# Layer 2's modulation on ScalarE and GpSimd over two stages, and every third low part of the weights on GpSimd

## The chip, the cores and the metric

The kernel runs on one core of a Trainium2 chip. The metric is the device time of one execution in microseconds (us); a group of runs is given by its median. The engines are TensorE (PE for its products, PEld for its weight loads), VectorE (DVE), ScalarE (ACT), GpSimd (POOL) and SyncE (SP, whose queue issues all the DMAs here). Each engine works through its own queue in order.

## What is computed

The reference is a two-layer encoder on 1024 tokens of width 1024. In each layer a modulation vector is made from the condition `c`; then come a norm, an input projection, four mixers side by side, an output projection, a second norm and a gated FFN with a short convolution:

```
cond = jax.nn.silu(c)
for l in range(DEPTH):                                  # 2 layers
    mod = cond @ ada_w[l] + ada_b[l]                    # 1024 -> 6 * 1024
    sh1, sc1, g1, sh2, sc2, g2 = jnp.split(mod, 6)
    h = _rms_norm(x, norm1_g[l]) * (1.0 + sc1) + sh1
    pa, pb, pc, pd = _split(h @ w_in[l], GROUP_COLS)
    y = concatenate([rwkv7(pa), diff_attention(pb), gating(pc), forgetting_attention(pd)])
    x = x + g1 * (y @ w_out[l])
    h = _rms_norm(x, norm2_g[l]) * (1.0 + sc2) + sh2
    x = x + g2 * _conv_glu_ffn(h, ffn_up[l], ffn_conv[l], ffn_conv_b[l], ffn_down[l])
```

All of it is float32.

## The kernel before

Tokens are worked on in two halves of 512 (`hf` 0 and 1), layer after layer. A main stage of one half (output projection `wout`, norm, FFN `ffn`, and the next input projection `win`) is written beside the mixers of the other half: `beside(main, mix, units)` takes so many steps of the mixers for each step of the main stage. Three such pairs follow each other: `rest(0,0)` and `win(1,0)` beside `mixers(0,1)`; `rest(0,1)` and `win(1,1)` beside `mixers(1,0)`; `rest(1,0)` beside `mixers(1,1)`. The last stage, `rest(1,1)`, runs alone. Layers are counted 0 and 1 in the code; in this text they are layer 1 and layer 2.

The order of writing gives priorities. The order in which each engine's queue is filled is made when the program is built, by a scheduler that goes through a simulated timeline; on the chip each engine then keeps to it.

**Weights (`wload`, line 491).** Every product of a main stage is made of three passes over weights split into a high part `wh` and a low part `wl` (`acc3`, line 471). One `wload` is a DMA into a raw buffer `wr` (two of them), a cast on ScalarE into `wh`, and a subtraction on VectorE into `wl`; both parts lie in the tile `hr`, three slots of 1024 columns each (`NW = 3`). A load is 1024 columns wide in the input and output projections and in the FFN's `up`, 512 or 384 in `down`.

**Modulation (`ada`, `adav`).** One layer's modulation is 12 groups of 512 outputs. A group is eight loads of 128x512 (`ar`, four buffers), each multiplied by a column of `cond` and summed. Layer 2's groups all go through `adav` (line 383): the even loads on VectorE (a multiplication, then three fused multiply-adds), the odd ones on GpSimd (four multiplications and three additions, lines 397 to 401), a sum of both on VectorE, four one-column products on TensorE into a `pn` tile, and a small addition (`adaout`). All 12 are written beside `rest(0,0)`, one step of a group at every second step of the FFN (`AEV = 2`), and what is left of them ahead of `win(1,0)`. The first norm of layer 2 reads groups 0 to 3, its output projection 4 and 5, its second norm 6 to 9, its FFN 10 and 11.

**Other work on GpSimd.** The FFN's gate has its product `ya * yg` (line 663) and the low part of its result `ml` (line 668) there; the norms have five additions; the mixers have a few clears, copies and parts of the rotation.

## Time and profile before

| | |
|---|---|
| time, median of 3 runs (lowest to highest) | 3023.8 us (3019.92 to 3026.89) |
| profiled execution, its own time | 3017.75 us |
| its span (first to last instruction) | 3016.0 us |
| mean granted TensorE clock, share of full speed | 0.963 |
| busy: PE, PEld, DVE, ACT, POOL | 95%, 80%, 69%, 45%, 20% |

The span is what the profile's views divide up; the profiled execution's own time is 1.75 us longer than it. A busy share is an average over stages that differ, so the views by window and the chain of work that ended last are read stage by stage. Busy time of TensorE counts pipelined products, so a busy TensorE is not one at its peak.

### The profile page before, as it was taken

To read this page: it belongs to the slowest core of one execution; us is meant where nothing else is said; L and a number is where in the kernel's file an instruction comes from. 1 tells how busy PE (TensorE), PEld (TensorE's weight loads), DVE (VectorE), ACT (ScalarE), POOL (GpSimd) and SP (SyncE) were. 2 spreads that over 40 slices of the span, in tenths; PEclk is the share of its full clock that TensorE was granted. 3 is DMA by queue.
4 is the path that set the end of the run, shared out by engine and by line. 5 is a ranking of instruction groups with operands and counts; after the bars stand their busy time and mean duration, and the time that the engine had idled before them with its cause. 6 is when DMAs were issued, how large, how long until landed. Compare 5 with 4: busy or idle time off the path is not lost.

```text
span 3016.0 us, 49828 instructions
## 1 busy us (share of the span) xinstructions
PE 2871.6 (95%) x17816; PEld 2419.6 (80%) x17816; DVE 2073.8 (69%) x4737; ACT 1361.4 (45%) x2760; POOL 609.2 (20%) x660
## 2 busy tenths in 40 slices
PE   7998989899889999999999999999999999999999
PEld 5987887777777888987888887888878888878887
DVE  4678777789886765668775665668787755565555
ACT  3455444444354544444644433455455445343333
POOL 2016253366511110100111111000111111111111
PEclk8999987989989999999999999999999999999999
DMA  7558455455532425463432324453332332523332
GB/s 271 146 164 292 154 169 181 136 163 175 181 98 70 142 85 168 144 188 112 128 109 94 98 75 160 147 170 115 104 113 76 118 109 90 187 59 110 111 95 73
DMA packets 276662, 405.78 MB, mean 135 GB/s; under 512 B 74560, under 2 KB 148800, under 8 KB 276416
## 3 DMA queue, kind: packets, MB, share of 16 engines
q1 hardware_dynamic: 276416, 402.61, 43.0%
q8 instruction: 141, 2.31, 0.3%
q14 instruction: 105, 0.86, 0.1%
HBM read 343.47 MB, written 59.02 MB: 133 GB/s over the span
## 4 chain that ended last, share of the span: by engine, by line
PE 75%; DVE 9%; DMA 7%; ACT 3%; issue 2%; SPq 2%; POOL 1%; DVEq 0%; ACTq 0%; POOLq 0%
PE pm L186 60%; PE pa L186 4%; PE px L186 4%; PE S L186 2%; PE px L1115 2%; DMA ar<-in_ada 2%; DVE hr L189 1%; DMA raw<-pA 1%; PE pn L186 1%; DVE cst L195 1%; DVE cst L189 1%; ACT hr L497 1%; SPq L980 1%; DMA qkB<-qh 1%; DVE cst L1093 1%
## 5 line engine op out<-in xcount | busy, mean ns | idle before, releaser
L186 PE MATMUL pm<-hh,hr 128*128 128x512 f32 (+1 forms) x3328 | 1091.1, 402 | 14.1 <-ACT hh L198 7.3
L186 PEld LDWEIGHTS pm<-hh,hr 128*128 128x128 f32 (+1 forms) x3328 | 627.2, 190 | 155.4 <-ACT hh L198 10.8
L497 ACT CAST hr<-wr 128x1024 fp32r<-128x1024 f32 (+2 forms) x496 | 427.1, 863 | 593.1 <-PE pm L186 484.0
L189 DVE TENSOR_TENSOR hr<-wr,hr 128x1024 fp32r<-128x1024 f32 (+2 forms) x496 | 515.1, 1039 | 249.9 <-ACT hr L497 232.8
L186 PE MATMUL pm<-hl,hr 128*128 128x512 f32 (+1 forms) x1664 | 666.8, 401 | 3.8 <-DVE hl L195 3.8
L186 PE MATMUL pm<-mh,hr 128*128 128x512 f32 x1408 | 460.2, 398 | 3.8 <-ACT p L198 2.8
L186 PE MATMUL pm<-hr,hh 128*128 128x256 f32 x2048 | 399.2, 291 | 7.4 <-DVE hr L189 6.0
L186 PEld LDWEIGHTS pm<-hl,hr 128*128 128x128 f32 (+1 forms) x1664 | 316.2, 190 | 72.5 <-DVE hl L195 6.6
L186 PEld LDWEIGHTS pm<-hr,hh 128*128 128x128 f32 x2048 | 325.6, 193 | 13.5 <-DVE hr L189 6.7
L663 POOL TENSOR_TENSOR y<-y,y 128x512 f32<-128x512 f32 x88 | 116.1, 1320 | 993.7 <-DVE y L189 335.2
L186 PEld LDWEIGHTS pm<-mh,hr 128*128 128x128 f32 x1408 | 266.0, 190 | 59.5 <-ACT p L198 3.3
L195 DVE SCALAR_TENSOR_TENSOR y<-pm,cst,y 128x511 f32<-128x511 f32 x352 | 261.1, 743 | 67.5 <-ACT y L198 64.1
L186 PE MATMUL pm<-hr,hl 128*128 128x256 f32 x1024 | 294.5, 288 | 0.0
L186 PE MATMUL pm<-ml,hr 128*128 128x512 f32 x704 | 277.1, 394 | 0.0
L195 DVE SCALAR_TENSOR_TENSOR x<-pm,cst,x 128x512 f32<-128x512 f32 x224 | 167.2, 747 | 138.3 <-PE pm L186 137.3
L198 ACT ACTIVATE p<-S,cst 128x512 f32<-128x512 f32 (+3 forms) x288 | 165.3, 580 | 90.8 <-DVE cst L189 66.5
L1093 DVE TENSOR_REDUCE cst<-S 128x1 f32<-128x512 f32 (+3 forms) x288 | 153.8, 550 | 70.1 <-PE S L186 69.0
L186 PEld LDWEIGHTS pm<-hr,hl 128*128 128x128 f32 x1024 | 198.1, 193 | 1.3 <-issue 0.7
L186 PEld LDWEIGHTS px<-V,ct 128*128 128x128 f32 x1152 | 160.0, 205 | 30.7 <-ACT ct L1117 22.0
L186 PE MATMUL px<-V,ct 128*128 128x64 f32 x1152 | 162.1, 285 | 17.9 <-ACT ct L1117 17.7
L186 PE MATMUL pm<-yh,hr 128*128 128x512 f32 x512 | 168.2, 405 | 3.9 <-ACT yh L621 3.1
L198 ACT ACTIVATE y<-pm,cst 128x512 f32<-128x512 f32 x176 | 136.6, 776 | 77.9 <-PE pm L186 77.5
(239 smaller groups left out, 3967.7 us busy)
## 6 DMA issues: line engine op xcount, KB each, us to landing
wr<-in_up SPq DMA_DIRECT2D x176, 512.0 KB
ar<-in_ada SPq DMA_DIRECT2D x192, 256.0 KB
wr<-in_wint SPq DMA_DIRECT2D x64, 512.0 KB
wr<-in_down SPq DMA_DIRECT2D x128, 256.0 KB
wr<-in_wout SPq DMA_DIRECT2D x32, 512.0 KB
wr<-in_win SPq DMA_DIRECT2D x28, 512.0 KB
ks<-qkB SPq DMA_DIRECT2D x192, 64.0 KB
wr<-in_down SPq DMA_DIRECT2D x64, 192.0 KB
```

The costliest lines, as they stand in the source:

```text
L186: return self.nc.tensor.matmul(out, lhsT, rhs, start=start, stop=stop, **kw)
L189: self.nc.vector.tensor_tensor(out=out, in0=a, in1=b, op=op)
L195: self.nc.vector.scalar_tensor_tensor(out=out, in0=a, scalar=s, in1=b, op0=op0, op1=op1)
L198: self.nc.scalar.activation(out=out, in_=in_, func=func, **k)
L497: self.nc.scalar.copy(out=h, in_=r)
L663: nc.gpsimd.tensor_tensor(out=ya, in0=ya, in1=yg, op=ALU.mult)
L980: nc.sync.dma_start(out=D[o:o + 16, :, c:c + 16], in_=XB[b0:b0 + 4].rearrange("b i t -> i b t"))
L1093: nc.vector.tensor_reduce(out=nm[:, i:i + 1], in_=S_[:, 0:n], axis=AX.X, op=ALU.max, negate=True)
L1115: nc.tensor.transpose(ps[:, j:j + 128], pc[:, j:j + 128], self.ident)
```

## The change

Three things are changed. Layer 2's groups go through a new `adaw`: all eight multiplications of a group on ScalarE and the seven additions on GpSimd, with one accumulator in place of two. The 12 groups are written in two stages: 0 to 3 beside `rest(0,0)` at every fifth step, 4 to 11 beside `rest(0,1)` at every second (`NA1, E1, E2 = 4, 5, 2`). And from the first of the three pairs to the end of the third (`K.lop = LOP` up to `K.lop = 0`), every third `wload` has its subtraction on GpSimd.

```
@@ -241,6 +241,7 @@
         self.identR, self.mDR, self.mBR = (hr[:, i * 128:i * 128 + 128] for i in range(3))
         self.wh, self.wl = ([hr[:, o + i * 1024:o + i * 1024 + 1024] for i in range(NW)] for o in (384, 384 + NW * 1024))
         self.nw = 0
+        self.npl, self.lop = 0, 0
         nc.vector.tensor_copy(self.identR, self.ident)
         for n, r in (("mD", self.mDR), ("mB", self.mBR)):
             t = self.ntile([128, 128], name="mt")
@@ -383,6 +384,9 @@
     def adav(self, l, g, pool, tag, apn):
 
         nc = self.nc
+        if l:
+            yield from self.adaw(l, g, pool, tag, apn)
+            return
         accs = [self.page(self.an, "an", [128, 512], F32, "av") for _ in range(2 if KD < 8 else 1)]
         new = [True, True]
         for kp in range(4):
@@ -407,6 +411,26 @@
             self.tt(accs[0], accs[0], accs[1], ALU.add)
         for u in range(4):
             self.mm(ps[:, u:u + 1], accs[0][:, u * 128:u * 128 + 128], self.ones[:, 0:1], True, True)
+        self.adaout(l, g, ps)
+
+    def adaw(self, l, g, pool, tag, apn):
+
+        nc = self.nc
+        acc = self.page(self.an, "an", [128, 512], F32, "av")
+        for k in range(8):
+            r = pool.tile([128, 512], F32, name="ar", tag=tag)
+            nc.sync.dma_start(out=r, in_=self.a["ada"][l, g, k // 2][:, k % 2 * 512:k % 2 * 512 + 512])
+            c = self.cond[:, k, 0:1]
+            if k == 0:
+                nc.scalar.mul(acc, r, c)
+            else:
+                nc.scalar.mul(r, r, c)
+                nc.gpsimd.tensor_tensor(out=acc, in0=acc, in1=r, op=ALU.add)
+            if k % 2:
+                yield
+        ps = (self.normps() if apn else self.pm.tile([128, H], F32, name="pm", tag="pm"))
+        for u in range(4):
+            self.mm(ps[:, u:u + 1], acc[:, u * 128:u * 128 + 128], self.ones[:, 0:1], True, True)
         self.adaout(l, g, ps)
 
     def adaout(self, l, g, ps):
@@ -495,7 +519,9 @@
         r = self.wr.tile([128, 1024], F32, name="wr", tag="wr")[:, 0:n]
         self.nc.sync.dma_start(out=r, in_=src)
         self.nc.scalar.copy(out=h, in_=r)
-        self.tt(lo, r, h.bitcast(F32), ALU.subtract)
+        self.npl += 1
+        e = self.nc.gpsimd if self.lop and self.npl % self.lop == 0 else self.nc.vector
+        e.tensor_tensor(out=lo, in0=r, in1=h.bitcast(F32), op=ALU.subtract)
         return h.rearrange("p (k c) -> p k c", k=nk), lo.rearrange("p (k c) -> p k c", k=nk)
 
     def product(self, w, acts, m=128):
@@ -1478,20 +1504,20 @@
                 side(oth, EARLY)
         drain(mix)
         xs[0] = K.load_x(0, True)
-        later = K.ada(1, range(NADA, 12), K.ar, "ar", APN)
-
-        def first():
-            for i, _ in enumerate(rest(0, 0)):
-                if i >= AST and (i - AST) % AEV == 0:
+        K.lop = LOP
+        def with_ada(main, groups, every):
+            later = K.ada(1, groups, K.ar, "ar", APN)
+            for i, _ in enumerate(main):
+                if i >= AST and (i - AST) % every == 0:
                     side(later, 1)
                 yield
             drain(later)
-            yield from win(1, 0)
-
-        beside(first(), K.mixers(0, 1, oth), U1)
+
+        beside(chain(with_ada(rest(0, 0), range(0, NA1), E1), win(1, 0)), K.mixers(0, 1, oth), U1)
         K.layer_params(1)
-        beside(chain(rest(0, 1), win(1, 1)), K.mixers(1, 0), U2)
+        beside(chain(with_ada(rest(0, 1), range(NA1, 12), E2), win(1, 1)), K.mixers(1, 0), U2)
         beside(rest(1, 0), K.mixers(1, 1), U3)
+        K.lop = 0
         K.out_x(0, xs[0])
         xs[1] = K.load_x(1)
         drain(rest(1, 1))
@@ -1500,6 +1526,8 @@
 
 U1, U2, U3 = 90, 60, 80
 MIX0 = 7
+NA1, E1, E2 = 4, 5, 2
+LOP = 3
 
 
 def chain(*gs):
```

How this stands in the queues is shown at three places. The first is ScalarE's queue where the FFN of layer 1 half 0 begins: `y_6773` and `y_6778` are the first pair of up products on their way out of PSUM, `hr` the casts of the weights, `p`, `ct`, `VS`, `yB` the mixers. Before:

```order
L198 ACTIVATE y_6773<-pm,cst 128x512
L497 CAST hr<-wr 128x1024
L198 ACTIVATE y_6778<-pm,cst 128x512
L892 COPY Y<-pa 128x128
L198 ACTIVATE th<-y_6778 128x512
L198 ACTIVATE gsq<-Y 128x256
L667 CAST mh<-th 128x512
L1117 COPY ct<-px 128x512
L1117 COPY ct<-px 128x256
L198 ACTIVATE p,cst<-S,cst 128x512
L198 ACTIVATE p,cst<-S,cst 128x384
L497 CAST hr<-wr 128x1024
```

And with the change, where the lines of the new function are 425 and 427, and the cast of the weights is line 521:

```order
L198 ACTIVATE y_6773<-pm,cst 128x512
L521 CAST hr<-wr 128x1024
L198 ACTIVATE y_6778<-pm,cst 128x512
L427 ACTIVATE ar<-ar,cst 128x512
L916 COPY VS<-pa 64x128
L427 ACTIVATE ar<-ar,cst 128x512
L198 ACTIVATE yB<-px,cst 128x64
L198 ACTIVATE p,cst<-S,cst 128x512
L198 ACTIVATE p,cst<-S,cst 128x256
L427 ACTIVATE ar<-ar,cst 128x512
L425 ACTIVATE av<-ar,cst 128x512
L198 ACTIVATE th<-y_6778 128x512
```

Multiplications of the modulation now stand between the drains of the products, the casts and the mixers' work.

The second place is GpSimd's queue at the same point, from one gate product (`y_6773`) on. Lines 397, 400 and 401 are the modulation before, 663 and 668 the gate. Before:

```order
L663 TENSOR_TENSOR y_6773<-y_6773,y_6778 128x512
L400 TENSOR_SCALAR ar<-ar,cst 128x512 x2
L668 TENSOR_TENSOR ml<-th,mh 128x512
L401 TENSOR_TENSOR av<-av,ar 128x512 x2
L400 TENSOR_SCALAR ar<-ar,cst 128x512
L397 TENSOR_SCALAR av<-ar,cst 128x512
L400 TENSOR_SCALAR ar<-ar,cst 128x512
L401 TENSOR_TENSOR av<-av,ar 128x512
L400 TENSOR_SCALAR ar<-ar,cst 128x512
L401 TENSOR_TENSOR av<-av,ar 128x512
L663 TENSOR_TENSOR y_6886<-y_6886,y_6916 128x512
```

With the change (line 428 is the modulation's addition, 524 the low part of a weight, 689 and 694 the gate):

```order
L689 TENSOR_TENSOR y_6773<-y_6773,y_6778 128x512
L428 TENSOR_TENSOR av<-av,ar 128x512
L694 TENSOR_TENSOR ml<-th,mh 128x512
L428 TENSOR_TENSOR av<-av,ar 128x512 x7
L524 TENSOR_TENSOR hr<-wr,hr 128x1024
L428 TENSOR_TENSOR av<-av,ar 128x512
L689 TENSOR_TENSOR y_6879<-y_6879,y_6909 128x512
L428 TENSOR_TENSOR av<-av,ar 128x512 x3
L694 TENSOR_TENSOR ml<-th,mh 128x512
```

The multiplications are gone from this queue, additions stand in their place, and a low part of the weights stands behind eight of them. Of the six groups that this order puts into the first stage, two stand ahead of the norm and four here; the other six are in the second stage.

The third place is GpSimd's queue in the FFN of layer 1 half 1. Before, it holds the gates alone:

```order
L663 TENSOR_TENSOR y_15350<-y_15350,y_15380 128x512
L668 TENSOR_TENSOR ml<-th,mh 128x512
L663 TENSOR_TENSOR y_15519<-y_15519,y_15549 128x512
L668 TENSOR_TENSOR ml<-th,mh 128x512
L663 TENSOR_TENSOR y_16233<-y_16233,y_16263 128x512
```

With the change it holds additions of layer 2's modulation between two gate products, and low parts among them:

```order
L689 TENSOR_TENSOR y_15283<-y_15283,y_15313 128x512
L428 TENSOR_TENSOR av<-av,ar 128x512
L694 TENSOR_TENSOR ml<-th,mh 128x512
L428 TENSOR_TENSOR av<-av,ar 128x512
L524 TENSOR_TENSOR hr<-wr,hr 128x512
L428 TENSOR_TENSOR av<-av,ar 128x512 x6
L524 TENSOR_TENSOR hr<-wr,hr 128x512
L428 TENSOR_TENSOR av<-av,ar 128x512 x6
L524 TENSOR_TENSOR hr<-wr,hr 128x1024
L428 TENSOR_TENSOR av<-av,ar 128x512 x7
L689 TENSOR_TENSOR y_16043<-y_16043,y_16073 128x512
```

Between these two gate products, 21 additions and three low parts have come in. In the whole order 117 low parts stand on GpSimd: 68 of 1024 columns, 32 of 512, 16 of 384 and one of 32.

## Rows read from the trace of the kernel before

**Rows 1.** The page of the kernel before, its first lines: the span, and for each engine the busy time, its share of the span and the number of instructions.

```profile
span 3016.0 us, 49828 instructions
PE 2871.6 (95%) x17816; PEld 2419.6 (80%) x17816; DVE 2073.8 (69%) x4737; ACT 1361.4 (45%) x2760; POOL 609.2 (20%) x660
```

**Rows 2.** The view by windows, all engines: us of the stretch, its length, then for PE, PEld, DVE, ACT and POOL the busy us (instructions), then the granted TensorE clock as a share of full speed, the DMA engines' busy share and GB/s. The stretches are output projection of layer 1 half 0 (482 to 559), the first and the second half of its FFN (559 to 850, 850 to 1145), the FFN of layer 1 half 1 (1395 to 1840), of layer 2 half 0 (2091 to 2595) and of layer 2 half 1 (2650 to 3016).

```profile
482.00:559.00 77.00, 73.50 (x508) 62.05 (x506) 56.83 (x137) 33.47 (x66) 19.97 (x19) 0.97 0.56 173
...
559.00:850.00 291.00, 261.89 (x1431) 213.34 (x1431) 260.24 (x528) 124.14 (x268) 157.92 (x103) 0.93 0.49 156
...
850.00:1145.00 295.00, 282.74 (x1749) 233.53 (x1748) 203.73 (x522) 144.44 (x318) 40.46 (x43) 0.97 0.36 107
...
1395.00:1840.00 445.00, 438.45 (x2530) 359.46 (x2530) 305.04 (x667) 207.72 (x411) 70.56 (x67) 0.99 0.35 109
...
2091.00:2595.00 504.00, 497.55 (x2925) 411.49 (x2926) 357.08 (x819) 251.46 (x526) 63.92 (x62) 0.98 0.36 109
...
2650.00:3016.00 366.00, 361.28 (x1584) 298.36 (x1584) 213.45 (x307) 132.75 (x185) 57.36 (x44) 0.99 0.30 90
```

**Rows 3.** The same view of one stretch inside the FFN of layer 2 half 0.

```profile
2100.00:2200.00 100.00, 98.00 (x556) 80.42 (x555) 81.64 (x194) 51.07 (x109) 14.13 (x14) 0.98 0.33 102
```

**Rows 4.** The view by windows of the instructions on the tile `pm` alone (the main products in PSUM and what drains them); columns PE, PEld, DVE, ACT, then clock, DMA share and GB/s.

```profile
559.00:850.00 291.00, 203.44 (x771) 148.49 (x771) 47.56 (x85) 18.02 (x24) 0.93 0.49 156
...
1395.00:1840.00 445.00, 387.38 (x1584) 293.27 (x1584) 100.50 (x135) 34.20 (x44) 0.99 0.35 109
...
2091.00:2595.00 504.00, 394.99 (x1585) 292.85 (x1586) 103.02 (x179) 34.10 (x44) 0.98 0.36 109
...
2650.00:3016.00 366.00, 361.28 (x1584) 298.36 (x1584) 101.75 (x136) 34.09 (x44) 0.99 0.30 90
```

**Rows 5.** The chain that ended last, its shares by line, in the stretches 559 to 850, 1395 to 1840 and 2091 to 2595, in this order.

```profile
by line: PE pm L186 23.8%; DMA ar<-in_ada 8.4%; issue 7.6%; DVE hr L189 6.9%; DVE cst L195 4.3%; DVE y L195 4.0%; PE px L186 2.8%; DVE av L403 2.7%; DVE cst L1093 2.6%; DVE cst L189 2.6%; PE pa L186 2.4%; DVE p L195 2.4%; POOL av L401 2.0%;
...
by line: PE pm L186 78.8%; PE pa L186 5.9%; PE px L186 3.1%; PE S L186 2.3%; PE px L1115 1.5%; DMA wr<-in_win 1.1%; issue 1.0%; DVE hl L195 0.7%; SPq L980 0.7%; DVE ht L195 0.6%; DVE hr L189 0.5%; DVE cst L189 0.5%; DMA D<-XB 0.4%; DVE x L1
...
by line: PE pm L186 68.2%; PE px L186 7.6%; PE pa L186 5.2%; PE S L186 4.8%; PE px L1115 3.5%; DMA wr<-in_wout 1.1%; DVE hl L195 1.0%; DVE hr L189 0.9%; issue 0.7%; DMA pc<-pC 0.7%; DVE ht L195 0.7%; DVE cst L1093 0.6%; DMA D<-XB 0.5%; DVE 
```

**Rows 6.** Pieces of that chain in the stretch 559 to 850, in order of time: start, us, what.

```profile
593.54 2.81 DMA ar<-in_ada
...
608.21 3.16 DMA ar<-in_ada
...
691.22 4.80 DMA ar<-in_ada
```

**Rows 7.** The instructions on the tiles `av` and `ar` (layer 2's modulation) and on `wr` (the weights as they land) in the stretch 559 to 850: line, engine, operation, tile, count, ns min/median/max of one, first and last start, forms.

```profile
L401 POOL TENSOR_TENSOR av<-av,ar x33: 1259/1374/2252, 562.7 to 825.7; 128x512 f32<-128x512 f32 x33
...
L403 DVE SCALAR_TENSOR_TENSOR av<-ar,cst,av x30: 735/748/1764, 592.8 to 819.5; 128x512 f32<-128x512 f32 x30
...
L397 POOL TENSOR_SCALAR av<-ar,cst x11: 1557/1643/2308, 561.1 to 806.8; 128x512 f32<-128x512 f32 x11
...
L189 DVE TENSOR_TENSOR av<-av x11: 675/679/1724, 586.2 to 830.5; 128x512 f32<-128x512 f32 x11
...
L397 DVE TENSOR_SCALAR av<-ar,cst x10: 441/474/777, 590.0 to 812.4; 128x512 f32<-128x512 f32 x10
...
L400 POOL TENSOR_SCALAR ar<-ar,cst x30: 1562/1615/3009, 570.9 to 822.6; 128x512 f32<-128x512 f32 x30
...
L189 DVE TENSOR_TENSOR hr<-wr,hr x42: 669/1208/2285, 558.2 to 846.5; 128x1024 fp32r<-128x1024 f32 x25, 128x512 fp32r<-128x512 f32 x17
```

**Rows 8.** Groups of instructions over the whole span, shapes apart: line, engine, operation, tiles, out<-in, count, then busy us and mean ns of one, then idle time of the engine just before them and what ended it. The first two are the low parts of the weights.

```profile
L189 DVE TENSOR_TENSOR hr<-wr,hr 128x1024 fp32r<-128x1024 f32 x300 | 374.4, 1248 | 227.6 <-ACT hr L497 212.5 <-ACT yD L198 5.4 <-PE px L1115 4.4
...
L189 DVE TENSOR_TENSOR hr<-wr,hr 128x512 fp32r<-128x512 f32 x128 | 101.5, 793 | 17.4 <-ACT hr L497 16.6
...
L663 POOL TENSOR_TENSOR y<-y,y 128x512 f32<-128x512 f32 x88 | 116.1, 1320 | 993.7 <-DVE y L189 335.2 <-DVE cst L657 329.5 <-ACT p L198 50.7
...
L198 ACT ACTIVATE sq<-x 128x512 f32<-128x512 f32 x88 | 54.7, 631 | 78.4 <-DMA x<-pD 32.6 <-DVE x L195 17.0 <-DMA x<-pB 15.5
...
L198 ACT ACTIVATE hh<-ht,cst 128x512 fp32r<-128x512 f32 x64 | 44.9, 722 | 49.5 <-DVE ht L195 43.3 <-DMA x<-in_xT 3.5 <-DVE cst L189 2.4
```

**Rows 9.** Waits in the stretch 559 to 850: the engine and line that waited, what for, us in total, times, longest. The two that begin with SPq are the DMA queue's own.

```profile
POOL ar L400 <- DMA ar<-in_ada: 54.1, 16, 11.7
...
PE pn L186 <- DVE av L189: 3.1, 3, 2.1
...
SPq L392 <- POOL av L401: 31.4, 17, 4.6
...
SPq L392 <- DVE av L403: 19.1, 11, 8.4
```

**Rows 10.** The largest wait of ScalarE's casts of the weights, over the whole span.

```profile
ACT hr L497 <- PE pm L186: 484.0, 258, 6.6
```

**Rows 11.** The timeline of TensorE at a modulation group's last four products (each in two passes) and what follows them: start, us, what.

```profile
577.22 0.95 PE L186 MATMUL pn<-cst,av 128*128 128x1 f32 x8
...
578.09 0.45 PE L186 MATMUL pa<-Us,Xs 64*64 64x64 f32 x8
```

**Rows 12.** One group of VectorE over the whole span that reads one operand from PSUM and one from SBUF, as a view by tile has it (count, ns min/median/max).

```profile
L195 DVE SCALAR_TENSOR_TENSOR x<-pm,cst,x x224: 717/751/753, 499.5 to 3012.4; 128x512 f32<-128x512 f32 x112
```

## The prediction

> **What bounds the kernel now.** I read the page first: TensorE is busy 95% of the span, VectorE 69%, ScalarE 45%, GpSimd 20% [rows 1]. So the first question is where TensorE's missing time lies. The view by windows answers it [rows 2]: in the FFN of layer 1 half 1 TensorE idles 445 - 438.5 = 6.5 us, in that of layer 2 half 0 504 - 497.6 = 6.4 us, in the last one 4.7 us. The first half of the first FFN, 559 to 850, is different: 291 - 261.9 = 29.1 us idle, the granted clock is 0.93 of full speed (so part of the stretch ran at 1.2 and not 2.4 GHz), and VectorE is busy 260.2 of 291 us, 89%. Layer 2's modulation runs there. The second half of that FFN has 12.3 us idle.
>
> The chain that ended last says the same [rows 5]. In the two later FFNs the main products hold 78.8% and 68.2% of it. In 559 to 850 they hold 23.8%; the loads of the modulation hold 8.4%, VectorE's low parts 6.9%, its share of the modulation 2.7%, GpSimd's 2.0%.
>
> What would that stretch take if only TensorE set the pace? The last FFN runs alone: 366 us for 1584 main products, 0.231 us each [rows 2, 4]. In the FFN of layer 2 half 0 the 1585 main products at that price take 366 us, and the other 2925 - 1585 = 1340 products the remaining 138 us, 0.103 us each. For 559 to 850 this gives 771 x 0.231 + 660 x 0.103 = 246 us. So some 45 us of 291 come from the other engines, and the change can win little elsewhere.
>
> **The change part by part.** The sum is made against the profiled execution, 3017.75 us; the runs' median, 3023.8 us, lies 6.05 us above it, and that is added at the end.
>
> *VectorE in 559 to 850.* The modulation leaves it: 30 x 0.748 + 10 x 0.474 + 11 x 0.679 = 34.6 us [rows 7]. Of 42 low parts (25 wide, 17 half) a third go: 8 x 1.248 + 6 x 0.793 = 14.7 us [rows 7, 8]. VectorE keeps 260.2 - 49.3 = 210.9 us.
>
> *TensorE there.* Of 96 one-column products, 64 move to the next stage with groups 4 to 11 (the order of the change has 4 groups' products ahead of layer 2's first norm). Eight take 578.09 - 577.22 = 0.87 us [rows 11], so 8 x 0.87 = 7 us leave: 246 becomes 239 us.
>
> *GpSimd there.* The modulation's 33 x 1.374 + 11 x 1.643 + 30 x 1.615 = 111.9 us go [rows 7]. Four groups' 28 additions come, 28 x 1.374 = 38.5 us, and 14 low parts. No GpSimd operation of 1024 columns is in the trace; the nearest, a two-input operation of 512, takes 1.320 us [rows 8]. The wide one lies between 1.3 (all of it fixed) and 2.64 us (none fixed). I take 2.64, as I see no fixed part: 8 x 2.64 + 6 x 1.32 = 29 us. GpSimd falls from 157.9 to 113.5 us. This engine is relieved too, for the four multiplications per group went to ScalarE.
>
> *ScalarE there.* Four groups bring 32 multiplications. Nearest rows: 0.631 us (one operand, constant scale) and 0.722 us (an operand per partition) [rows 8]; I take the second, as `cond` is such an operand: 23 us on top of 124.1.
>
> *What this gives.* VectorE's 210.9 us need room: the highest share it has beside a TensorE at 98% is 81.6% [rows 3], and 210.9 / 0.816 = 258 us. That is later than TensorE's 239, so VectorE still paces the stretch, and I get 33 us of the 45. Something is given back on ScalarE: its queue now meets the modulation's loads itself. GpSimd waited 54.1 us for them over its 41 multiplications [rows 7, 9], 1.3 us each; 32 on ScalarE are up to 42 us. Behind each wait stand casts of weights and drains of products. ScalarE has 258 - 147 = 111 us idle, so I let one fifth reach the path, 8 us. Term: **-25 us**, bounds -52 (TensorE's price) and -6 (below).
>
> *482 to 559.* Two groups' 16 multiplications (11.6 us on ScalarE, busy 33.5 of 77) and 14 additions (19 us) with three low parts on GpSimd stand ahead of the norm's additions. **+2 us**, 0 to +8: the norm waits at most for the end of that row.
>
> *850 to 1145.* VectorE loses the low parts of a third of the weights, at most 17 x 1.248 = 21 us of 203.7. Idle is 12.3 us [rows 2]. **-3 us**, -8 to 0.
>
> *The FFN of layer 1 half 1.* TensorE is full there, and 7 us of one-column products come to it. In the first FFN TensorE waited 3.1 us for three of the sums [rows 9]; here the sum is GpSimd's, at the end of a queue. GpSimd gets 42 x 1.374 = 58 us of additions, and between two gate products 21 of them with three low parts: 21 x 1.374 + 2.64 + 2 x 1.32 + 1.32 = 35.5 us, while the eight `down` products of that place take TensorE 8 x 12 x 0.231 = 22 us and the mixers beside them more. A low part behind such additions can be late by up to 13 us. VectorE, relieved by some 28 us, gives back nothing that TensorE waits for (its low parts hold 0.5% of the chain [rows 5]). **+8 us**, 0 to +22.
>
> *The other low parts.* 117 subtractions leave VectorE in all. A cast into a slot waits for TensorE to finish with it, 484.0 us in 258 waits [rows 10]; the two other slots are full then, 2 x 24 x 0.231 = 11 us of products for wide loads, 5.5 us in `down`. A wide low part later by 2.64 - 1.25 = 1.4 us, a half one by 0.5 us, is hidden by that. If a norm or a pair of products empties the slots, it costs the 1.4 us, some four times. **0 us**, -5 to +8.
>
> Sum: -25 + 2 - 3 + 8 + 0 = -18; 3017.75 - 18 = 2999.75, and with 6.05 **3005.8 us**.
>
> **The rivals.**
>
> *The queues of ScalarE and GpSimd hold the products (slower).* A low part of the weights stands in GpSimd's queue behind additions, these wait for ScalarE, which waits for a load; a load took 2.8 to 4.8 us on the chain [rows 6], and its buffer comes free only with the addition. For it: the SP queue waited 31.4 us for GpSimd's additions [rows 9], and the order has up to seven additions ahead of a low part. Against it: GpSimd has less to do in 559 to 850 than before. Price: two thirds of ScalarE's 42 us reach the path there, 27 us in place of 8 (term -6), and the other ends are +8, 0 for 850 to 1145 and +22: +24 with the rest at 0, 3017.75 + 24 + 6.05 = 3047.8 us. It is slower than before from about 18 us of such waits beyond my own terms.
>
> *VectorE isn't what holds 559 to 850.* Its busy share is then only company, and the pace comes from loads and from round trips of the mixers: "issue" and loads hold 7.6 and 8.4% of the chain, more than VectorE's low parts and modulation together (9.6%). Then only part of the modulation's own chain goes: -10 + 2 + 0 + 8 = 0, 3023.8 us.
>
> *The shared port.* VectorE's operations with two operands in SBUF are stretched when GpSimd runs: the fused multiply-add on `av` has a median of 0.748 and a maximum of 1.764 us, while one that reads PSUM and SBUF has 0.751 and 0.753 [rows 7, 12]. The stretch, 1.0 us, is within a GpSimd operation of 1.3; one of 2.64 us could hold VectorE twice as long. If each of the 117 takes back on average what it relieves, VectorE keeps 225.6 us in 559 to 850, 225.6 / 0.816 = 276 us: -15 + 8 = -7 there, and the small operations of the mixers, held up to 2.6 us, cost 4 us in each later FFN: -7 + 2 + 0 + 8 + 8 = +11, 3034.8 us. The Trainium skill, page "SBUF — State Buffer", section "Who interferes with whom", has this as its rule: a GpSimd operation that reads SBUF and a VectorE operation with two SBUF inputs lock each other out for a whole instruction. By that rule the time is this rival's; the two maxima agree with it. Against the price: GpSimd's total busy time falls in the one stretch where VectorE is short.
>
> *All of the 45 us.* TensorE sets the pace in 559 to 850 (-52), 850 to 1145 gives -8, the second stage costs +5: -55, 2968.8 us. For it: a faster stretch also has the clock that it lacks (0.93 against 0.98).
>
> **How the numbers follow.** Forecast 0.42, queues 0.22, not VectorE 0.15, port 0.08, all of it 0.13. The likeliest is the forecast, 3006 us, alone 2990 to 3020. The range of 8 in 10 reaches into the neighbours: down to 2980 (most of the last rival lies below) and up to 3034 (half of the first rival and half of the port's above). About 0.2%, 6 us, is what a measurement of this kernel can tell from no change: faster is below 3017.8, slower above 3029.8. Faster: 0.38 of the forecast, 0.13, and 0.04 of "not VectorE", 0.55. Slower: 0.20 of the queues and 0.05 of the port, 0.25. The rest, 0.20, is the same.
>
> **What would show it.** In the profile of the changed kernel the stretch from the first `up` product, as long as 1431 - 64 products, should take some 266 us with VectorE at 79% and TensorE's idle time near 12 us. The wide low part on GpSimd should take 2.6 us; at 2.0 us the queue rival weakens. ScalarE's multiplications should idle some 30 to 40 us for loads. The FFN of layer 1 half 1 should take some 453 us; at 465 us, with TensorE waiting for `hr` released by GpSimd, the first rival holds. VectorE's small operations at 1 us and more would speak for the port. The prediction is wrong if the first FFN keeps its 586 us, or if the second stage loses what the first wins.

## The result and the profile after

| kernel | median | runs | ratio to before |
|---|---|---|---|
| before | 3021.9 us | 4 (3016.1 to 3026.9) | 1 |
| changed | 3060.1 us | 4 (3057.6 to 3065.2) | 1.013 [1.0109, 1.015] |

Slower by 38 us; 3006 was forecast, with 3034 as the upper end. The profiled run has a span of 3060.3 us, 44.3 more than before. First the head of the page after; it answers to [rows 1].

```profile
span 3060.3 us, 49880 instructions
...
PE 2880.4 (94%) x17816; PEld 2419.2 (79%) x17816; DVE 2025.3 (66%) x4560; ACT 1418.3 (46%) x2856; POOL 815.3 (27%) x777
```

VectorE did lose work, but less than was taken from it. At the prices of [rows 7, 8], an estimate, layer 2's modulation is some 41 us on VectorE and the 100 larger low parts are 110 us; its busy time fell by 48.5 (2073.8 to 2025.3 us). GpSimd gained 206 us. The same view by windows as in [rows 2], for the stretches that answer to those: output projection and norm, first FFN up to 850 and as a whole, norm and input projection of layer 2 half 0, FFN of layer 1 half 1, FFN of layer 2 half 0.

```profile
494.00:581.00 87.00, 80.97 (x511) 66.62 (x509) 57.87 (x129) 31.03 (x58) 26.35 (x23) 0.89 0.48 148
581.00:850.00 269.00, 251.38 (x1409) 205.12 (x1407) 210.16 (x469) 150.14 (x317) 98.64 (x71) 0.97 0.41 124
...
581.00:1137.00 556.00, 526.25 (x3091) 431.13 (x3090) 408.76 (x959) 287.69 (x617) 169.14 (x130) 0.97 0.39 114
1137.00:1324.00 187.00, 172.22 (x1287) 154.44 (x1286) 107.97 (x267) 87.40 (x171) 31.75 (x24) 0.94 0.51 161
1405.00:1876.00 471.00, 451.27 (x2582) 367.68 (x2580) 307.76 (x635) 231.65 (x452) 180.15 (x139) 0.98 0.41 125
2133.00:2638.00 505.00, 495.57 (x2931) 407.91 (x2930) 355.39 (x791) 248.49 (x526) 115.94 (x92) 0.99 0.36 108
```

The first FFN gained what was forecast: 556 us for 585 (559 to 1144 in before), -29. The rest lost 73: +12 up to the output projection (its order is changed too, and the first low part of GpSimd starts at 431.9 us), +10 in it and its norm, +16 in 1137 to 1324, +28 in the FFN of layer 1 half 1 (471 us for the 443 from 1395 to 1838), +7 in the others together. Inside that FFN the loss lies in its first 150 us. The same view there:

```profile
1405.00:1430.00 25.00, 19.02 (x113) 15.43 (x112) 22.26 (x44) 13.64 (x29) 9.19 (x8) 0.81 0.61 176
1475.00:1500.00 25.00, 18.40 (x84) 13.99 (x84) 24.66 (x51) 10.32 (x23) 13.76 (x10) 0.91 0.31 94
1500.00:1525.00 25.00, 25.00 (x150) 20.66 (x150) 13.71 (x31) 17.61 (x37) 18.48 (x14) 0.95 0.61 189
1525.00:1550.00 25.00, 20.54 (x97) 16.62 (x96) 24.84 (x46) 15.66 (x26) 18.66 (x13) 0.93 0.59 203
1550.00:1575.00 25.00, 25.00 (x126) 21.15 (x125) 16.48 (x34) 12.91 (x29) 9.01 (x6) 1.00 0.45 129
```

Where TensorE is short, VectorE is full (24.66 and 24.84 of 25 us) with only 51 and 46 operations; in before it had 77 in a window of 25 us as full, and TensorE was hardly short:

```profile
1475.00:1500.00 25.00, 24.32 (x118) 19.89 (x117) 24.94 (x77) 12.67 (x29) 2.61 (x2) 1.00 0.30 89
```

Of TensorE's waits in 1405 to 1555, 18.1 of 20.2 us are for steps of VectorE, of the FFN (`y`), a norm and the mixers, and none for weights. The three longest (what it waited for, us in total, times, longest):

```profile
PE pm L186 <- DVE y L189: 6.1, 1, 6.1
PE pa L943 <- DVE Y L189: 4.1, 1, 4.1
PE pa L186 <- DVE cst L189: 3.1, 1, 3.1
```

VectorE's and GpSimd's rows of the timeline there (start, us, what):

```profile
1481.14 1.31 POOL L428 TENSOR_TENSOR av<-av,ar 128x512 f32<-128x512 f32 x1
...
1481.24 1.22 DVE L195 SCALAR_TENSOR_TENSOR cst<-cst 128x4 f32<-128x4 f32 x1
...
1482.40 1.30 POOL L524 TENSOR_TENSOR hr<-wr,hr 128x512 fp32r<-128x512 f32 x1
...
1482.72 2.23 DVE L189 TENSOR_TENSOR cst<-cst 128x4 f32<-128x4 f32 x2
...
1484.99 0.16 DVE L195 SCALAR_TENSOR_TENSOR cst<-cst 128x4 f32<-128x4 f32 x1
...
1487.86 6.34 POOL L428 TENSOR_TENSOR av<-av,ar 128x512 f32<-128x512 f32 x4
...
1487.96 3.45 DVE L189 TENSOR_TENSOR Vn<-Vn,cst 128x512 f32<-128x512 f32 x2
```

The same multiply-add of four columns takes 1.22 us at 1481.24, beside an addition of GpSimd, and 0.16 at 1484.99, where GpSimd rests. Two `Vn` products, 0.745 us each on average in before, take 3.45 beside GpSimd's additions, and the FFN's `y`, for which a TensorE product waited 6.1 us until 1496.3, stands behind such products in VectorE's queue. So VectorE is held up: its operations take longer beside GpSimd's. But `Vn` is held as long with no low part on GpSimd (982 ns on average in e1 below, 996 here), so these rows don't tell which part of the change costs the 38 us. The groups over the whole span, shapes apart; they answer to [rows 7, 8]:

```profile
L524 DVE TENSOR_TENSOR hr<-wr,hr 128x1024 fp32r<-128x1024 f32 x232 | 297.6, 1283 | 210.5 <-ACT hr L521 197.0 <-ACT yD L198 6.3 <-PE px L1141 3.6
...
L524 POOL TENSOR_TENSOR hr<-wr,hr 128x1024 fp32r<-128x1024 f32 x68 | 165.4, 2432 | 635.6 <-ACT hr L521 590.9 <-PE pm L186 34.7 <-PE S L186 9.9
...
L428 POOL TENSOR_TENSOR av<-av,ar 128x512 f32<-128x512 f32 x84 | 115.5, 1375 | 95.6 <-ACT av L425 65.6 <-ACT ar L427 26.0 <-PE pm L186 0.3
...
L427 ACT ACTIVATE ar<-ar,cst 128x512 f32<-128x512 f32 x84 | 59.4, 723 | 51.9 <-DMA ar<-in_ada 51.0 <-POOL av L428 0.7
...
L524 POOL TENSOR_TENSOR hr<-wr,hr 128x512 fp32r<-128x512 f32 x32 | 43.7, 1366 | 86.0 <-ACT hr L521 69.6 <-PE S L186 16.1 <-POOL Xs L1029 0.2
```

### The profile page after: what moved, and what is told of

Its sections match the earlier page's. It is cut to its first block, busy times and chain, and to the rows that moved or that the text cites. A ratio compares the mean times of both kernels' runs of the same rounds, so it can differ in the third digit from the quotient of the medians.

```text
span 3060.3 us, 49880 instructions
## 1 busy us (share of the span) xinstructions
PE 2880.4 (94%) x17816; PEld 2419.2 (79%) x17816; DVE 2025.3 (66%) x4560; ACT 1418.3 (46%) x2856; POOL 815.3 (27%) x777
## 4 chain that ended last, share of the span: by engine, by line
PE 69%; DVE 12%; DMA 8%; ACT 4%; issue 2%; SPq 2%; POOL 2%; ACTq 0%; DVEq 0%; POOLq 0%
PE pm L186 56%; PE pa L186 4%; PE px L186 4%; PE S L186 2%; PE px L1141 2%; DVE hr L524 2%; DVE cst L189 1%; DMA ar<-in_ada 1%; ACT hr L521 1%; DMA raw<-pA 1%; POOL av L428 1%; DMA wr<-in_win 1%; DVE y L195 1%; PE pn L186 1%; DVE cst L195 1%
## 5 line engine op out<-in xcount | busy, mean ns | idle before, releaser
L524 DVE TENSOR_TENSOR hr<-wr,hr 128x1024 fp32r<-128x1024 f32 (+2 forms) x379 | 403.8, 1066 | 237.0 <-ACT hr L521 223.1
L524 POOL TENSOR_TENSOR hr<-wr,hr 128x1024 fp32r<-128x1024 f32 (+3 forms) x117 | 226.8, 1938 | 784.9 <-ACT hr L521 716.6
L189 DVE TENSOR_TENSOR cst<-cst 128x1 f32<-128x1 f32 (+5 forms) x552 | 135.5, 255 | 74.4 <-ACT p L198 62.2
```

Of the source, the lines that this page charges most:

```text
L189: self.nc.vector.tensor_tensor(out=out, in0=a, in1=b, op=op)
L524: e.tensor_tensor(out=lo, in0=r, in1=h.bitcast(F32), op=ALU.subtract)
```

## The experiments

In the table below, all times are against runs of the kernel before on the same chip (3018.7 to 3022.4 us).

| run | what it is | us | ratio |
|---|---|---|---|
| e1 | new modulation in two stages, no low part on GpSimd | 3023.6 | 1.0011 [0.9993, 1.003] |
| e2 | old modulation, low parts on GpSimd | 3055.2 | 1.0119 [1.0096, 1.0143] |
| e3 | new modulation, one stage | 3021.1 | 0.9997 [0.9981, 1.0012] |
| e4 | old modulation, two stages | 3019.1 | 0.9996 [0.9979, 1.0013] |
| f1 | e1, GpSimd only waits at the cast | 3019.9 | 1.0002 [0.9986, 1.0017] |
| f2 | e1, GpSimd reads and subtracts beside | 3053.9 | 1.0106 [1.0081, 1.0131] |
| h1 | e1, GpSimd writes instead | 3012.9 | 0.9972 [0.9954, 0.9989] |
| f3 | changed, low parts in halves | 3015.7 | 0.9981 [0.9968, 0.9993] |
| h2 | changed, low parts in quarters | 3018.3 | 0.9985 [0.9969, 1.0001] |
| h3 | as f3, second half first | 3036.5 | 1.0053 [1.0034, 1.0071] |
| g1 | e2 with halves | 3031.2 | 1.0039 [1.0027, 1.0052] |
| g2 | f3, the modulation's additions in halves too | 3015.7 | 0.9998 [0.9985, 1.0011] |
| g4 | f2 with halves | 3048.1 | 1.0095 [1.008, 1.011] |
| f4 | e1, multiplications and additions on 8 columns | 2990.0 | 0.9902 [0.988, 0.9924] |
| g3 | e1, additions alone on 8 columns | 3009.2 | 0.9958 [0.9942, 0.9973] |

**Which part costs.** Four kernels with one part each.

```diff
e1  -LOP = 3
    +LOP = 0
e2  -NA1, E1, E2 = 4, 5, 2        (and adav runs its old form in layer 2 too)
    +NA1, E1, E2 = 12, 2, 2
e3  -NA1, E1, E2 = 4, 5, 2        -LOP = 3
    +NA1, E1, E2 = 12, 2, 2       +LOP = 0
e4  -LOP = 3                      (and adav runs its old form in layer 2 too)
    +LOP = 0
```

In the expectations, theory S blames the second stage, L the low parts on GpSimd, O the new order of the queues.

Expected of e1: 

> The changed kernel without the low parts on GpSimd (all on VectorE again): the new modulation in two stages alone. Theory S (the second stage is the cause: layer 2's additions on GpSimd and its multiplications on ScalarE in the full FFN of layer 1 half 1 hold VectorE's small operations and the casts): it stays slow, 3050 to 3060 us, and the FFN of layer 1 half 1 takes some 470 us as in the changed kernel. Theory L (the low parts on GpSimd are the cause): it is faster than before, some 3005 us, with that FFN at 445 to 455 us. Theory O (a new order of all queues moves time at places that the change does not touch): 3020 to 3050 us, with the loss spread over stretches without modulation.

Of e2: 

> The kernel before with every third low part on GpSimd and nothing else. Theory S: 3010 to 3025 us, since GpSimd's low parts hide behind the slots; the FFN of layer 1 half 1 at 445 us. Theory L: 3040 to 3060 us. Theory O: within 15 us of before either way, with the difference in the projections and norms more than in the FFNs.

Of e3: 

> The new modulation (multiplications on ScalarE, additions on GpSimd) for all 12 groups in the first stage at every second step, as before, and no low parts on GpSimd: the engines alone. Theory S: faster than before, 2995 to 3010 us, since the first FFN is relieved on VectorE by 35 us and the second stage is left alone. Theory L says the same. If the multiplications on ScalarE are themselves the cause (its queue waits for the loads), it is 3030 us or more with the first FFN at 585 us or longer.

Of e4: 

> The old modulation (VectorE and GpSimd) written in two stages, 0 to 3 and 4 to 11, and no low parts on GpSimd: the split alone. Theory S with the stage as the cause whatever the engine: 3035 to 3055 us, the FFN of layer 1 half 1 at 465 us or more. If it is the new engines in the full stage and not the stage: 3010 to 3025 us. Theory L: 3005 to 3020 us.

The low parts alone (e2) cost 1.2%, about all of the 1.3; the modulation in either form and place costs and gains nothing. So theory S falls, and O by e2, which it had put within 15 us of before. L is right about what costs, but not about the rest: it had expected e1 at some 3005 us and e3 at 2995 to 3010, and the gain that the low parts were thought to hide isn't there. Where that comes from shows in the starts of ScalarE's 496 casts of weights, of which every kernel has the same; the figures are us later (+) or earlier (-) than in before:

```
cast number     64     96    128    160    192    224    288    480
start before   628    827   1038   1230   1471   1636   1942   2965
changed      +16.6   +4.4  -10.7   -4.9  +17.5  +37.5  +41.8  +44.4
e1           +16.5   +1.2  -21.3  -23.7  -15.4   +3.3   +4.6   +4.3
e2           +10.5  +12.1   -6.4   +0.9  +22.2  +31.8  +28.1  +41.6
e4            +6.2  -15.3  -43.7  -37.2  -27.4   -4.3   -8.2   -4.1
f4           +14.3  -14.6  -37.6  -39.8  -35.2  -25.3  -24.0  -26.9
```

With the modulation in two stages e1 and e4 are 24 and 44 us ahead after the first FFN, and from there to cast 224 they give back 27 and 39. The low parts (changed against e1) take 40 us, 30 of them from cast 96 to 192.

**Queue, or the reading.** In f1 VectorE makes each low part, and GpSimd copies one column of the cast in its place, so that its queue stops there as before. In f2 GpSimd makes a subtraction of the low part's shape that no product needs, and in h1 it fills the same spare tile twice.

```diff
-        e = self.nc.gpsimd if self.lop and self.npl % self.lop == 0 else self.nc.vector
-        e.tensor_tensor(out=lo, in0=r, in1=h.bitcast(F32), op=ALU.subtract)
+        self.tt(lo, r, h.bitcast(F32), ALU.subtract)
+        if self.lop and self.npl % self.lop == 0:
f1 +            self.nc.gpsimd.tensor_copy(out=self.pk, in_=h.bitcast(F32)[:, 0:1])
f2 +            self.nc.gpsimd.tensor_tensor(out=self.sp[:, 0:n], in0=r, in1=r, op=ALU.subtract)
h1 +            self.nc.gpsimd.tensor_copy(out=self.sp[:, 0:1], in_=r[:, 0:1])
h1 +            for _ in range(2):
h1 +                self.nc.gpsimd.memset(self.sp[:, 0:n], 0.0)
```

The lines that make the spare tiles `pk` and `sp` are left out here.

Expected of f1: 

> VectorE makes every low part again; at the place of every third one GpSimd copies one column of the cast weights into a spare column, so that its queue waits for ScalarE's cast as in the changed kernel, but then works some 0.1 us and not 2.4. The modulation stays as changed. Theory P (a low part of 1024 columns on GpSimd holds up VectorE's operations with two operands in SBUF): as the kernel without low parts on GpSimd, 3024 us, 3018 to 3030. Theory Q (GpSimd's queue, in order, stands at the low part until the cast is done, and what is behind it comes late): 3045 to 3060. Theory D (the low part itself reaches TensorE 1.2 us later): 3024.

Of f2: 

> VectorE makes every low part again; for every third load GpSimd subtracts the loaded tile from itself into a spare tile, with the shape of the low part, which nobody waits for but the buffer of the load. The modulation stays as changed. Theory P: GpSimd's 227 us of such subtractions hold VectorE as before, and VectorE keeps its own 117 low parts: 3050 to 3075 us. Theory Q: GpSimd stands at a load and no longer at a cast: 3024 to 3032. Theory D: 3024.

Of h1: 

> VectorE makes all low parts. For every third load GpSimd copies one column of the loaded tile (so that it waits for the load as in the run with the subtraction of the tile from itself, 3054 us), and then fills a spare tile of the load's width twice, about as long as that subtraction, reading nothing. The modulation stays as changed. Theory P3 (it is GpSimd's reading from SBUF that VectorE's operations with two SBUF operands stand behind): as without low parts on GpSimd, 3018 to 3030 us. Rival T (GpSimd's occupied time as such: its own later operations are late, and the scheduler orders the rest of the program around it): 3045 to 3060.

f1 is as before, although GpSimd stood 802.0 us at the casts in it: theory Q (the queue) falls.

```profile
L526 POOL COPY cst<-hr 128x1 f32<-128x1 f32 x117 | 74.8, 639 | 813.4 <-ACT hr L522 802.0 <-PE pa L186 6.5 <-PE px L186 2.5
```

f2 costs 1.06% although VectorE still made the low parts and no product waits for GpSimd's result. h1 has the same place and about the same time on GpSimd, and costs nothing; at 3012.9 us it lies even below its expectation. GpSimd's groups, f2 first, then h1:

```profile
L526 POOL TENSOR_TENSOR cst<-wr 128x1024 f32<-128x1024 f32 x68 | 135.9, 1998 | 556.8 <-DMA wr<-in_up 263.0 <-DMA wr<-in_wint 155.6 <-DMA wr<-in_wout 58.8
L526 POOL TENSOR_TENSOR cst<-wr 128x512 f32<-128x512 f32 x32 | 38.0, 1187 | 60.8 <-DMA wr<-in_down 48.7 <-DVE cst L685 11.9
```

```profile
L528 POOL MEMSET cst<- 128x1024 f32 x136 | 129.7, 954 | 7.2
L528 POOL MEMSET cst<- 128x512 f32 x64 | 33.7, 526 | 3.3
```

With the smaller shapes that is 190 us of subtractions, which read, against 177 us of fills, which do not: 3053.9 and 3012.9 us. The busy time of VectorE shows what the reading does. The engines' lines of the pages of e1, f2 and h1, in which VectorE has the same 4677 instructions:

```profile
PE 2872.2 (95%) x17816; PEld 2418.9 (80%) x17816; DVE 2040.5 (68%) x4677; ACT 1424.1 (47%) x2858; POOL 596.6 (20%) x660
```

```profile
PE 2874.5 (94%) x17816; PEld 2417.9 (79%) x17816; DVE 2137.2 (70%) x4677; ACT 1420.3 (47%) x2856; POOL 779.3 (26%) x777
```

```profile
PE 2859.8 (95%) x17816; PEld 2408.3 (80%) x17816; DVE 2046.8 (68%) x4677; ACT 1420.4 (47%) x2856; POOL 796.4 (26%) x1011
```

The subtractions lengthen VectorE's work by 97 us, the fills by 6. In f2 TensorE waited 39 us more for VectorE than in e1, and the span is 33 us longer. So it is the reading (theory P3), and not GpSimd's time.

Two differences between f2 and h1 besides the reading could be rivals. f2 keeps the load's buffer until its subtraction is done; but the casts waited less for loads in f2 (54 us) than in e1 (66) and in h1 (127), each summed over the rows of their waits. And h1's fills are half as long, 954 ns; but with subtractions of 1218 ns, in the run g4 below, the kernel still takes 3048.1 us.

Theory D (low parts that come late to TensorE) falls by the changed kernel's waits. Over its whole span TensorE's products waited 0.7 us for a low part of GpSimd, and 90 of 175 us for VectorE:

```profile
PE px L1141 <- DVE p L195: 18.0, 5, 6.2
PE pm L186 <- DVE cst L189: 15.4, 6, 6.5
...
PE pm L186 <- POOL hr L524: 0.7, 2, 0.3
```

(Of the second row, 9.3 us lie in the first 50 us of the program, before any low part on GpSimd.) Against e1 the span of the changed kernel is 40 us longer: TensorE waited 24 us more for VectorE, 15 more for ScalarE, 4 more for GpSimd and 13 less for loads, and its products were busy 8 us longer. So VectorE's share is the largest, but here, other than in f2, it isn't all; that the waits for ScalarE come from VectorE too isn't shown.

**The length of one operation.** In f3 two subtractions of half the columns stand in place of GpSimd's one; h2 and h3 differ from it in the loop alone.

```diff
f3  +            for c0 in (0, n // 2):
    +                cs = slice(c0, c0 + n // 2)
    +                self.nc.gpsimd.tensor_tensor(out=lo[:, cs], in0=r[:, cs], in1=h.bitcast(F32)[:, cs], op=ALU.subtract)
h2  +            for c0 in range(0, n, n // 4):        h3  +            for c0 in (n // 2, 0):
```

g1 is e2 with f3's loop, g4 is f2 with its subtraction in two halves, and g2 is f3 with the modulation's additions as two of 256 columns each.

Expected of f3: 

> The changed kernel with each low part of GpSimd made as two subtractions of half the columns. Theory P, if one VectorE operation loses at most the rest of one GpSimd operation: the hold is 1.3 and not 2.4 us, the loss of 36 us about halves, 3036 to 3046. Theory Q and theory D: the same wait and the same end plus some 0.1 us, 3056 to 3064.

Of h2: 

> The changed kernel with GpSimd's low parts as four subtractions of 256 columns (192 and 128 or less in the loads for the down products); in one piece it was 3060, in two 3016. Theory P3 with a hold that grows with the length of one operation: 3008 to 3018 us. If the number of GpSimd operations that can collide counts against it: 3018 to 3035. Rival T: above 3016 by the added fixed time on GpSimd, 3025 to 3040.

Of h3: 

> The changed kernel with GpSimd's low parts in two halves, the second half first, so that a product has to wait for both halves as it did for the whole. If the halves won since a product, on the chip or in the scheduler's plan, may begin after the first: 3045 to 3060 us. Theory P3: 3010 to 3024.

Of g1: 

> The kernel before with every third low part on GpSimd, each as two subtractions of half the columns (in one piece these cost 33 us: 3055). Theory P2 (what costs is the length of one GpSimd operation, which a VectorE operation of the mixers stands behind): the halves win here what they won with the new modulation, 44 us, or at least half of it: 3012 to 3033 us. Rival R (the halves only led the scheduler to a luckier order in that one kernel): 3044 to 3060.

Of g4: 

> The run in which GpSimd subtracts every third loaded tile from itself into a spare tile and VectorE keeps all low parts (3054 us), with that subtraction in two halves. Theory P2: the price of 30 us at least halves: 3022 to 3038. Rival T, and a buffer of the load that is held longer: 3050 to 3060.

Of g2: 

> The changed kernel with GpSimd's low parts in halves (3016 us), and now the modulation's additions of 512 columns as two of 256 too. Theory P2: they were 1.4 us and become about 0.8; with 8 columns (0.1 us and less time on ScalarE too) the gain was 33 us, so a third to a half of that: 2999 to 3008. Rival T (it is GpSimd's total time, which rises with more pieces): 3015 to 3025.

One VectorE group of the mixers, with two operands in SBUF, shows the hold, that is, how much longer an operation takes beside GpSimd's: count, then ns min/median/max. The fences are of the changed kernel, f2, f3 and h1, in this order; before had 339/741/1786.

```profile
L195 DVE SCALAR_TENSOR_TENSOR p<-p,cst x96: 338/742/2881, 194.1 to 2363.9; 128x512 f32<-128x512 f32 x48, 128x128 f32<-128x128 f32 x16, 128x256 f32<-128x256 f32 x16, 128x384 f32<-128x384 f32 x16
```

```profile
L195 DVE SCALAR_TENSOR_TENSOR p<-p,cst x96: 334/742/2251, 194.8 to 2351.9; 128x512 f32<-128x512 f32 x48, 128x128 f32<-128x128 f32 x16, 128x256 f32<-128x256 f32 x16, 128x384 f32<-128x384 f32 x16
```

```profile
L195 DVE SCALAR_TENSOR_TENSOR p<-p,cst x96: 336/744/1859, 200.8 to 2311.0; 128x512 f32<-128x512 f32 x48, 128x128 f32<-128x128 f32 x16, 128x256 f32<-128x256 f32 x16, 128x384 f32<-128x384 f32 x16
```

```profile
L195 DVE SCALAR_TENSOR_TENSOR p<-p,cst x96: 333/742/1861, 197.8 to 2306.3; 128x512 f32<-128x512 f32 x48, 128x128 f32<-128x128 f32 x16, 128x256 f32<-128x256 f32 x16, 128x384 f32<-128x384 f32 x16
```

The median stays; the maximum, which one or two of the 96 reach, goes with the mean length of GpSimd's longest reading operations (2.43 us, 2.00, 1.37, and 1.4 in h1, which keeps the 512-column additions). The halves win 44 us in f3 and 24 in g1, though GpSimd's time rises. f3 came out 20 us below its lowest expectation, and VectorE didn't get its time back in it: its busy time is 2017.9 us, 7 less than in the changed kernel. So the halves don't lessen what VectorE loses; it is cut into shorter holds, and TensorE waited 74.2 us for VectorE in place of 89.9. Four runs fit this less well. h3, between its two expectations, keeps 24 of the 44, so the other 20 hang on the first half being made first: either a product's earlier start in the scheduler's plan, or the order that came of it. In g4 the maximum fell to 1873 ns and TensorE's waits for VectorE from 104.7 to 79.8 us (summed over the rows of that view), but its waits for ScalarE rose from 41.6 to 70.7, and 6 us were left of the gain (3 against its own runs of before); theory P2 wanted at least 16. In g2 the additions in halves won nothing, where P2 wanted 8 to 17 us. And quarters (h2) are no better than halves. Kernels with whole pieces (the changed one, e2, f2) are 1.1 to 1.3% slower than before, and those with halves or quarters lie from 0.2% below to 0.95% above it. That the length of a piece counts is likely, then, but not shown by itself, and how much it counts stays open.

**Why the modulation won nothing.** f4 and g3 keep all of e1's loads, instructions and products, with narrow operations; they leave out the sums of the other columns, so they measure a price and are no kernels to use.

```diff
-                nc.scalar.mul(r, r, c)
-                nc.gpsimd.tensor_tensor(out=acc, in0=acc, in1=r, op=ALU.add)
f4 +                nc.scalar.mul(r[:, 0:8], r[:, 0:8], c)
g3 +                nc.scalar.mul(r, r, c)
f4, g3 +                nc.gpsimd.tensor_tensor(out=acc[:, 0:8], in0=acc[:, 0:8], in1=r[:, 0:8], op=ALU.add)
```

Expected of f4: 

> No low part on GpSimd. Layer 2's modulation as changed, over two stages, with all its loads, instructions and products in their places, but the multiplications and additions of all but the first row block work on 8 of 512 columns (the rest of the modulation is left out). The modulation's place wins 21 us in the first FFN and loses 25 us in the second stage. If the time of its operations on ScalarE and GpSimd costs that (holding VectorE or standing ahead of casts): 2998 to 3008 us. If its loads and what waits in the queues for them cost it: 3018 to 3028.

Of g3: 

> No low part on GpSimd; the modulation over two stages with ScalarE's multiplications on all 512 columns, and GpSimd's additions on 8 (the rest of the sums is left out). Both narrow was 2990, both wide 3024. If GpSimd's additions cost it (theory P2): 2990 to 3002. If ScalarE's multiplications ahead of the casts cost it: 3014 to 3024.

f4 is 33.6 us below e1, and 8 below its lowest expectation: the loads and their queues do not hold the modulation's price, its wide operations do. f4 also gives back 12 us between casts 128 and 224, where e1 gives back 25. g3, between its two expectations, gives 14.4 of the 33.6 to GpSimd's additions, so 19.2 to ScalarE's multiplications; against their own runs of before it is 16 and 17 us, about half each. How the multiplications cost it no run shows. TensorE's waits for VectorE, summed over the rows of the view of its waits, and one small VectorE operation follow roughly what GpSimd reads:

| | GpSimd's reading beside the mixers | TensorE waits for VectorE | `cst<-cst` 128x1, 194 of it: mean ns |
|---|---|---|---|
| before | old modulation | 74.0 us | 216 |
| g3 | least | 47.5 us | 177 |
| e1 | + the additions | 65.6 us | 197 |
| e3 | + the additions, in one stage | 78.5 us | 238 |
| h1 | as e1, and fills | 55.7 us | 196 |
| f3 | + low parts, halves | 74.2 us | 236 |
| changed | + low parts, whole | 89.9 us | 262 |
| e2 | old modulation, whole low parts | 91.4 us | 265 |
| f2 | as e1, and whole subtractions | 104.7 us | 253 |

The three kernels with whole pieces stand highest. Below them the steps say little: e1 and e3 make the same additions and lie 13 us and 41 ns apart.

## Why the prediction was wrong

*VectorE in 559 to 850, -25.* Right, and in the main with its mechanism. 266 us were forecast for 1367 products (1431 - 64); from 581 to 850, 269 us, the changed kernel made 1409. VectorE's 210.16 us stand against 210.9 forecast, and its share is 78% against 79%. TensorE's idle time was 17.6 us for 12. One part came otherwise: ScalarE's multiplications idled 6.6 us for loads there, where I had let up to 42 us of waits give 8 us back.

*482 to 559, +2 (0 to +8).* Mis-sized: +10. e1 has the delay too (+16.5 at cast 64, the changed kernel +16.6), so the low parts are not its cause; and f3 and h1, with the same modulation, have +2.6 and +3.6 there, so it belongs more to the order than to the modulation. The norm's additions, which I named, are not all of it, for TensorE waited 6.2 us for them in the whole span.

*850 to 1145, -3.* Together with the first stretch -28 was forecast for the FFN, and -29 came.

*The FFN of layer 1 half 1, +8 (0 to +22).* Mis-sized: +28. The step that failed is "VectorE, relieved by some 28 us, gives back nothing that TensorE waits for". I had put the risk into low parts late behind additions, on the way to the product; TensorE waited 0.7 us for those. What is late there is VectorE, whose operations take longer beside GpSimd's (18.1 of TensorE's 20.2 us of waits in the first 150 us). The low parts are not all of it: e1 loses 25 us between casts 128 and 224 without a single one on GpSimd, and f4, with narrow operations, 12. So the moved groups won nothing, since their place was only changed from one stretch that VectorE paces to the start of another.

*The other low parts, 0 (-5 to +8).* **This step failed.** They cost 33 us (e2) to 37 (changed against e1). The argument was about the weights' own path, and there it held. What this term left out is what a reading GpSimd operation does to VectorE: in e2 the 100 larger low parts, 110 us at the prices of [rows 8], left VectorE, and its busy time fell by 32 us (2073.8 to 2041.5).

*The rivals.* The shared port was the right mechanism as far as the runs show one, at a chance of 0.08, and priced at +11 in the sum where the run shows +44. Its condition, that each low part takes back on average what it relieves, came out nearly so (e2 took back some 78 of 110 us). But I let the additions' relief in 559 to 850 pay for it and gave each later FFN 4 us, and the sign that I had named for it, small VectorE operations of 1 us and more, is in the timeline (1.22 us at 1481.24). The rule of the Trainium skill, page "SBUF — State Buffer", section "Who interferes with whom" (a GpSimd operation that reads SBUF stands against a VectorE operation with two inputs in SBUF, one that only writes doesn't), agrees with f2 and h1, 1.0106 against 0.9972. "The queues of ScalarE and GpSimd hold the products" came nearest in time (3047.8), by luck: f1 refutes its mechanism for GpSimd's queue, and e1, whose ScalarE queue meets the same loads, for ScalarE's. "VectorE isn't what holds 559 to 850" gave the time of e1 and e3, 3024 and 3021 us, but not by its mechanism: in e1 the stretch did get shorter, and the time went later.

What stays open: why VectorE's lost time costs 40 us in the changed kernel and nothing in f3, which loses nearly as much of it; the missing gains of g4 and g2; and by how much the scheduler's order alone moves such a kernel. Kernels with an edit that should be neutral (e1, e3, e4, f1, h1) lay between 0.9972 and 1.0011, so differences below some 0.4% between two of these orders say little. f3, the best kernel with the low parts on GpSimd, is 0.2% faster than before, within that spread, and 1.5% faster than the change.

## What to carry to other kernels

GpSimd is no free place for two-input elementwise work beside code whose chains run through VectorE: price its reading as VectorE's time, and look in the stretch to which it goes, not in the one that it leaves. If it must go there, try it in pieces no longer than the operations that GpSimd already has, and measure: this won 44, 24 and some 5 us in three kernels. Work that is moved between stages wins only if the engine that it loads has room in the new one; compare the progress of both kernels at the same step of the program, and a gain that is given back later shows at once.

## What the hardware showed

- GpSimd's subtraction of 1024 columns takes 2432 ns and of 512 columns 1366: 2.08 ns per column and 0.3 us fixed.
- VectorE's two-input operations in SBUF were stretched, at most by less than one GpSimd operation (742 ns median, 2881 maximum beside 2432 ns). A scaling of one SBUF tile (`Vn`, 128x256) was stretched too: 407 ns on average in e1, 404 in h1, 533 in f2, 719 in the changed kernel. A reciprocal of 128x1 kept its 156 to 160 ns in before, changed, f2 and h1, and the operation of [rows 12], with one input in PSUM, its maximum of 753 ns in the changed kernel.
- 177 us of fills on GpSimd beside the same mixers cost nothing measurable.
- GpSimd's queue standing at a wait cost nothing by itself: it stood 802.0 us at the casts in f1 (1.0002 of before).
